# Attention scores on one core: TensorE's unrolled program becomes a loop over two tiles, with operands copied to fixed places by GpSimd

## The chip, the cores and the metric

The kernel runs on one core of a Trainium2 chip. A core has a matrix engine (TensorE, PE in the profile; PEld is its weight load), VectorE (DVE), ScalarE (ACT), GpSimd (POOL) and SyncE (SP), which here only issues transfers and passes counts on. Sixteen DMA engines move data between the chip's memory (HBM) and the core's on-chip memory SBUF. PE writes its results to a second on-chip memory, PSUM. The engines run programs of their own and wait for each other through semaphores, which are counters. The metric is the time of one execution in microseconds on the device, lower is better.

## The reference

```python
batch, heads, seq, dim = 8, 8, 512, 64
def reference(q, k):
    scale = 1.0 / np.sqrt(q.shape[-1])
    return (np.einsum('bhqd,bhkd->bhqk', q, k) * scale).astype(np.float32)
```

For each of 64 heads, the 512x64 queries are multiplied by the 512x64 keys, transposed, and scaled. The inputs are 16.8 MB in float32 and the output is 67.1 MB in float32, so the kernel reads little and writes much.

## The kernel before

**Units, chunks and tiles.** The eight batches are taken two at a time, in four *units* v. A unit's keys and queries are one load of 2 MB each (x = 0 for keys, x = 1 for queries). A unit has four *chunks* c: two of keys, two of queries, eight 128x128 blocks each, which PE transposes. A unit also gives four *tiles* g of output, 4 MB each: 16 tiles in all, and 16 chunks in all.

**The stages.** SP issues the loads into three large buffers, `bigs` (`load`, lines 81 and 82; the very first load is cut in two halves, one of them issued by ACT). POOL casts a loaded half-block from float32 to bfloat16 into `xb`, a ring of 12 chunk places (line 131; 16 casts of 128x2048). The bfloat16 pairs are then treated as float32 words, so that a transpose moves two values at once. PE transposes chunk c with an identity matrix as the moving operand into the PSUM tile `tp` (`turn`, line 139). ACT and DVE move the transposed chunk into `kT` (keys) and `qz` (queries, with zeros around them), each one half of the partitions in two copies (`move`, line 193). Both have places for two units.

**A tile.** `scores(g, p)` is one pair of matmuls (line 154): 128 query rows against 512 keys, bfloat16, into one of three PSUM buffers `pss`, taken in turn by the running number of the pair. A tile has eight pairs p. ACT takes the even pairs out of PSUM, DVE the odd ones, both multiplying by the scale, into the store buffer (lines 218 and 221, 128x1024 each). SP waits until both are through with the tile (line 101) and stores it (line 102). The store buffers are the same three `bigs` that the loads use.

**Order on PE.** The program is written out in full: four transposed chunks first, then 16 tiles. In tile g, after three pairs, PE transposes chunk g + 4 (there are 12 such chunks), then comes back to the other five pairs. Every matmul's addresses are written into its instruction: the place in `qz` and `kT` by g modulo 8, the PSUM buffer by the pair's number modulo 3. The second matmul of a tile's first pair waits for the store that last used the tile's output buffer, or, for the first three tiles, until POOL has cast what the buffer still holds:

```python
if g < 3:
    pe.wait_ge(sem["ready"], (2, 6, 8)[g])
else:
    pe.wait_ge(store_sems[g % 3], g // 3 * 16)
```

**What is counted.** `ready` counts pairs of casts, `turn` transposed chunks, `moved` the copies out of `tp`, `pe_act` and `pe_dve` pairs finished by PE, `act` and `dve` pairs taken out. A pair waits for the pair three before it to have left PSUM.

Of the kernel before, what the change touches and what calls it, by code (L numbers as in the profile page):

```python
# [5 lines left out]
def kernel(  # L6
# [5 lines left out]
    nc = tc.nc  # L12
    B, H, S, D = q.shape
    scale = 1.0 / (D ** 0.5)
    P = 128
    UNITS = B // 2
    N = H
    M = P // (2 * H)
    R = S // M
    J = R // 2  # L20
    RO = 8
    U = S // RO
    JP = J // 2
    JJ = J // RO // 2
    W = 8
    IW = W // JJ
    TILES = N // 2
    CHUNKS = 4
    SLOTS = 12
    PAIRS = RO  # L30

    f32 = mybir.dt.float32
    bf16 = mybir.dt.bfloat16
    mult = mybir.AluOpType.mult


    names = ["ready", "moved", "zeroed", "ident", "turn", "pe_act", "pe_dve", "act", "dve"]
    sem = {name: nc.alloc_semaphore(name) for name in names}
    load_sems = [nc.alloc_semaphore(f"load{n}") for n in range(2 * UNITS)]
    halves = [load_sems[0], nc.alloc_semaphore("load0b")]  # L40
    store_sems = [nc.alloc_semaphore(f"store{n}") for n in range(3)]
    ALL = CHUNKS * UNITS
# [2 lines left out]
    k_r = k.rearrange("(v b) g (m j) d -> v (b g m) (j d)", b=2, j=R)  # L45
    out_r = out.rearrange("(v b) (t x h) (u i) k -> (v b t) (h u) x (i k)", b=2, x=2, h=2, i=RO)

    bigs = [nc.alloc_sbuf_tensor(f"big{n}", [P, 2, RO, S], f32)[:] for n in range(3)]
    xb = nc.alloc_sbuf_tensor("xb", [P, SLOTS * W, 2, D, 2], bf16)[:]
    kT = nc.alloc_sbuf_tensor("kT", [P, 2 * N, M, 2, J], bf16)[:]  # L50
    qz = nc.alloc_sbuf_tensor("qz", [P, 2 * N, RO, P], bf16)[:]
    identity = nc.alloc_sbuf_tensor("identity", [P, P], f32)[:]
    tp = nc.alloc_psum_tensor("tp", [P, W, P], f32)[:]
    pss = [nc.alloc_psum_tensor(f"ps{n}", [P, 2, S], f32)[:] for n in range(3)]

    def words(ap):
        return ap.bitcast(f32)

    def half(h):
        return slice(h * D, (h + 1) * D)  # L60

    kw = words(kT)
    qw = words(qz)
    xw = words(xb.rearrange("p w s d e -> p w (s d e)"))
    keys = kT.rearrange("p n m s j -> p n (m s j)")

    pe = nc.tensor

    def xf(v):
        return bigs[(0, 1, 2, 1)[v]].rearrange("p x i k -> p (x i k)").rearrange(
            "p (x s c) -> p x s c", x=2, s=2)

    def store_buffer(g):
        return bigs[(0, 2, 1)[g % 3]]

    def rows(v, x):
        return (k_r, q_r)[x][v].rearrange("p (s c) -> p s c", s=2)

    def load(v, x):
        nc.sync.dma_start(out=xf(v)[:, x], in_=rows(v, x)).then_inc(load_sems[2 * v + x], 16)
# [8 lines left out]
    tc.compile()  # L91


    for n in range(1, 2 * (UNITS - 1)):
        load(n // 2, n % 2)
    for x in range(2):
        nc.sync.wait_ge(sem["ready"], 3 + x)
        load(UNITS - 1, x)
    for g in range(ALL):
        nc.sync.wait_ge(sem["act"], 4 * g + 4)  # L100
        nc.sync.wait_ge(sem["dve"], 4 * g + 4)  # L101
        nc.sync.dma_start(out=out_r[g], in_=store_buffer(g).rearrange("p x i k -> p x (i k)")
                          ).then_inc(store_sems[g % 3], 16)
    for n in range(3):
        nc.sync.wait_ge(store_sems[n], 16 * len(range(n, ALL, 3)))


    nc.gpsimd.memset(identity, 0.0).then_inc(sem["ident"], 1)  # L108
# [2 lines left out]
                            fill=1.0, base=0, pattern=[[-1, P]], channel_multiplier=1  # L111
                            ).then_inc(sem["ident"], 1)
    for v in range(UNITS):
        for x in range(2):
            w0 = (v * CHUNKS + 2 * x) % SLOTS * W
            if v or x:
                nc.gpsimd.wait_ge(load_sems[2 * v + x], 16)
            if v == UNITS - 1 and x == 0:
                nc.gpsimd.wait_ge(sem["turn"], CHUNKS)
            for s in range(2):  # L120
                if v == x == 0:
                    nc.gpsimd.wait_ge(halves[s], 16)
                src = xf(v)[:, x, s]
                dst = xb[:, w0:w0 + JP, s]
                if x == 0:
                    src = src.rearrange("p (j e d) -> p j e d", e=2, d=D)
                    dst = dst.rearrange("p j d e -> p j e d")
                else:
                    src = src.rearrange("p (j e i d) -> p j e i d", e=2, i=RO, d=D)
                    dst = dst.rearrange("p (i j) d e -> p j e i d", i=RO)  # L130
                cast = nc.gpsimd.tensor_copy(out=dst, in_=src)  # L131
            cast.then_inc(sem["ready"], 1)


    first = [tp] + [ps.rearrange("p w (c k) -> p (w c) k", k=P) for ps in pss]

    def turn(c, dst):
        for w in range(W):
            ins = pe.transpose(out=dst[:, w], identity=identity, in_=xw[:, c % SLOTS * W + w])  # L139
        ins.then_inc(sem["turn"], 1)  # L140

    def scores(g, p):
        x, i = p // 4, p % 4 * 2
        n = g % (2 * TILES) * 2 + x
        pair = PAIRS * g + p
        if pair >= 3:
            pe.wait_ge(sem["act" if p % 2 else "dve"], (pair - 3) // 2 + 1)
        for w in range(2):
            if p == 0 and w == 1:
                if g < 3:  # L150
                    pe.wait_ge(sem["ready"], (2, 6, 8)[g])
                else:
                    pe.wait_ge(store_sems[g % 3], g // 3 * 16)
            ins = pe.matmul(out=pss[pair % 3][:, w, :], lhsT=qz[:, n, i + w], rhs=keys[:, n],  # L154
                            start=True, stop=True)
        ins.then_inc(sem["pe_dve" if p % 2 else "pe_act"], 1)

    pe.wait_ge(sem["ident"], 2)
    for c in range(CHUNKS):
        if c % 2 == 0:  # L160
            pe.wait_ge(sem["ready"], c // 2 + 1)
        turn(c, first[c])
    pe.wait_ge(sem["moved"], 4 * CHUNKS)
    for g in range(ALL):
        c = g + CHUNKS
        for p in range(3):
            scores(g, p)
        if c < ALL:
            pe.wait_ge(sem["ready"], c // 2 + 1)
            turn(c, tp)  # L170
        for p in range(3, PAIRS):
            scores(g, p)
        if c < ALL:
            pe.wait_ge(sem["moved"], 4 * c + 4)

    def move(copy, c, s, tile_):
        v, t = divmod(c, CHUNKS)
        n0 = v % 2 * N  # L180
        h0 = t % 2 * W
        if t < 2:
            src = tile_[half(s)].rearrange("d j (n h m) -> d h n m j", n=N, h=2)
        else:
            src = tile_[half(s)].rearrange("d (i jj) (n h m) -> d h i n m jj", jj=JJ, n=N, h=2)
            h0 = t % 2 * IW
        for h in range(2):
            if t < 2:
                dst = kw[half(h), n0:n0 + N, :, s, h0:h0 + W]
            else:  # L190
                dst = qw[half(h), n0:n0 + N, h0:h0 + IW, h * U // 2:(h + 1) * U // 2].rearrange(
                    "d n i (m s jj) -> d s i n m jj", s=2, jj=JJ)[:, s]
            copy(out=dst, in_=src[:, h]).then_inc(sem["moved"], 1)  # L193

    def evacuator(engine, copy, scaled, parity, done, freed):
        if parity:
            for v in range(2):
                engine.memset(qz[:, v * N:(v + 1) * N], 0.0).then_inc(sem["zeroed"], 1)  # L198
        for c in range(CHUNKS):
            engine.wait_ge(sem["turn"], c + 1)  # L200
            if c == 2:
                engine.wait_ge(sem["zeroed"], 2)
            move(copy, c, parity, first[c])
        count = 0
        for g in range(ALL):
            o = store_buffer(g)
            for p in range(parity, PAIRS, 2):
                x, i = p // 4, p % 4 * 2
                count += 1
                engine.wait_ge(done, count)  # L210
                scaled(o[:, x, i:i + 2, :], pss[(PAIRS * g + p) % 3]).then_inc(freed, 1)
                c = g + CHUNKS
                if p in (1, 2) and c < ALL:
                    engine.wait_ge(sem["turn"], c + 1)
                    move(copy, c, parity, tp)

    evacuator(nc.scalar, nc.scalar.copy,
              lambda o, ps: nc.scalar.mul(out=o, in_=ps, mul=scale),  # L218
              0, sem["pe_act"], sem["act"])
    evacuator(nc.vector, nc.vector.tensor_copy,  # L220
              lambda o, ps: nc.vector.tensor_scalar(out=o, in0=ps, scalar1=scale, scalar2=None,  # L221
                                                    op0=mult),
              1, sem["pe_dve"], sem["dve"])


# [28 lines left out]
```

## Time and profile before

| | us |
|---|---|
| median of 5 runs | 201.21 (201.12 to 201.32) |
| the profiled execution's own time | 201.28 |
| its span, first to last instruction | 200.0 |
| PE busy in matmuls (384) | 101.2 |
| DVE busy (98 instructions) | 106.0 |
| ACT busy (97) | 84.8 |
| POOL busy (22) | 39.4 |
| DMA, mean over the span | 420 GB/s, 83.95 MB |

The profile's first part gives each engine's busy time, the second cuts the span into 40 slices of 5 us and gives busy tenths of each engine and of the 16 DMA engines together. The third lists the DMA queues: each line has a queue's packets, its megabytes and the time of its packets as a share of 16 engines' span. Queue q1 holds what SP issued, q10 what ACT issued, and the queues marked "instruction" fetch program code. The other parts list groups of instructions with their mean duration and what ended the idle time before them, waits, and DMA issues. The same questions can be put to any stretch of the span; "marks" below are the small completion packets that each transfer leaves, one for each DMA engine.

### The profile page before, as it was taken

What the parts mean: (1) busy time and instruction counts of PE and PEld (TensorE: products, weight loads), DVE (VectorE), ACT (ScalarE), POOL (GpSimd) and SP (SyncE); (2) the same over time, 40 slices, a digit from 0 to 9 for tenths busy, and PEclk for the clock granted to TensorE, in tenths of its full rate; (3) what the DMA queues carried; (4) which work ended last, traced back from release to release, by engine and by line L of the source; (5) the groups of instructions that cost most, each with busy time, mean ns of one, the idle gap of its engine ahead of it and who ended that gap; (6) DMA issues with size and microseconds to landing.
All of it is one profiled execution on the core that took longest, in us unless ns stands there. A gap on an engine that the chain in (4) does not pass through costs nothing.

```text
span 200.0 us, 1082 instructions
## 1 busy us (share of the span) xinstructions
PE 101.2 (51%) x384; PEld 47.3 (24%) x384; DVE 106.0 (53%) x98; ACT 84.8 (42%) x97; POOL 39.4 (20%) x22
## 2 busy tenths in 40 slices
PE   0027660476875767654764587365737373830000
PEld 0036430143331424312431333041202020200000
DVE  4815691176895847691769276829364544450000
ACT  2004670265693646562665366446444343430000
POOL 1299999996000000000000000000000000000000
PEclk9999997579797888995899579969696968585555
DMA  5999999999999999999999999999999999999995
GB/s 195 451 426 436 426 423 439 426 390 433 436 436 423 429 434 438 423 423 439 423 433 429 433 436 433 426 429 436 433 429 419 436 433 433 426 423 439 433 433 256
DMA packets 5653, 83.95 MB, mean 420 GB/s; under 512 B 400, under 2 KB 400, under 8 KB 400
## 3 DMA queue, kind: packets, MB, share of 16 engines
q1 hardware_dynamic: 5504, 82.84, 97.3%
q10 hardware_dynamic: 144, 1.05, 1.3%
q8 instruction: 3, 0.05, 0.1%
q14 instruction: 2, 0.02, 0.0%
HBM read 16.78 MB, written 67.11 MB: 419 GB/s over the span
## 4 chain that ended last, share of the span: by engine, by line
DMA 56%; DVE 12%; PE 10%; POOL 10%; issue 1%; SPq 0%
DMA out_dram<-big 42%; DMA big<-in_q_dram 13%; POOL xb L131 10%; DVE big L221 10%; PE ps L154 7%; PE tp L139 3%; DVE qz L193 2%; DVE kT L193 1%; SPq L101 0%
## 5 line engine op out<-in xcount | busy, mean ns | idle before, releaser
L154 PE MATMUL ps<-kT,qz 128*128 128x512 bf16 x256 | 81.0, 454 | 60.6 <-DMA out_dram<-big 30.7
L221 DVE TENSOR_SCALAR big<-ps 128x1024 f32<-128x1024 f32 x64 | 76.9, 1222 | 52.4 <-PE ps L154 51.9
L218 ACT ACTIVATE big<-ps 128x1024 f32<-128x1024 f32 x64 | 65.0, 1023 | 71.3 <-PE ps L154 70.9
L154 PEld LDWEIGHTS ps<-kT,qz 128*128 128x128 bf16 x256 | 25.1, 110 | 109.6 <-DMA out_dram<-big 34.4
L131 POOL CAST xb<-big 128x2048 bf16<-128x2048 f32 x16 | 38.7, 2464 | 6.6 <-DMA big<-in_k_dram 5.9
L139 PE MATMUL tp<-identity,xb 128*128 128x128 f32 x104 | 19.2, 347 | 13.5 <-POOL xb L131 13.5
L139 PEld LDWEIGHTS tp<-identity,xb 128*128 128x128 f32 x104 | 17.5, 187 | 17.5 <-issue 16.3
L193 DVE COPY kT<-tp 64x512 f32<-64x512 f32 x14 | 9.7, 694 | 9.8 <-PE tp L139 9.4
L193 ACT COPY kT<-tp 64x512 f32<-64x512 f32 x14 | 8.1, 577 | 14.4 <-PE tp L139 14.1
L193 DVE COPY qz<-tp 64x512 f32<-64x512 f32 x12 | 8.3, 695 | 3.8 <-PE tp L139 3.4
L198 DVE MEMSET qz<- 128x4096 uint32 x2 | 6.9, 3472 | 3.6 <-PEq L91 2.8
L193 ACT COPY qz<-tp 64x512 f32<-64x512 f32 x12 | 7.4, 618 | 1.7 <-PE tp L139 1.6
L139 PE MATMUL ps<-identity,xb 128*128 128x128 f32 x24 | 5.6, 423 | 1.2 <-POOL xb L131 1.2
L139 PEld LDWEIGHTS ps<-identity,xb 128*128 128x128 f32 x24 | 5.0, 229 | 1.6 <-POOL xb L131 1.6
L193 DVE COPY qz<-ps 64x512 f32<-64x512 f32 x4 | 2.8, 695 | 2.1 <-PE ps L139 2.0
L193 ACT COPY qz<-ps 64x512 f32<-64x512 f32 x4 | 2.5, 625 | 2.5 <-PE ps L139 2.4
L193 ACT ACT_TABLE_LOAD x1 | 1.3, 1283 | 1.9 <-PEq L91 1.9
L193 DVE COPY kT<-ps 64x512 f32<-64x512 f32 x2 | 1.4, 694 | 0.3 <-PE ps L139 0.3
L193 ACT COPY kT<-ps 64x512 f32<-64x512 f32 x2 | 1.2, 578 | 0.5 <-PE ps L139 0.5
L108 POOL MEMSET identity<- 128x128 f32 x1 | 0.2, 204 | 1.5 <-POOLq L91 1.5
L110 POOL TENSOR_SCALAR_AFFINE_SELECT identity<-identity 128x128 f32<-128x128 f32 x1 | 0.3, 292 | 0.2 <-POOL identity L108 0.2
L238 POOL MEMSET const-float32-0.0<- 128x1 f32 x1 | 0.1, 98 | 0.2 <-issue 0.2
(3 smaller groups left out, 0.3 us busy)
## 6 DMA issues: line engine op xcount, KB each, us to landing
out_dram<-big SPq DMA_DIRECT2D x16, 4096.0 KB, 21.3
big<-in_q_dram SPq DMA_DIRECT2D x4, 2048.0 KB, 17.6
big<-in_k_dram SPq DMA_DIRECT2D x3, 2048.0 KB, 16.0
big<-in_k_dram ACTq DMA_DIRECT2D x1, 1024.0 KB, 7.9
big<-in_k_dram SPq DMA_DIRECT2D x1, 1024.0 KB, 7.8
```

Source lines behind the costliest of these rows:

```text
L108: nc.gpsimd.memset(identity, 0.0).then_inc(sem["ident"], 1)
L110: nc.gpsimd.affine_select(out=identity, in_=identity, compare_op=mybir.AluOpType.not_equal, fill=1.0, base=0, pattern=[[-1, P]], channel_m ...
L131: cast = nc.gpsimd.tensor_copy(out=dst, in_=src)
L139: ins = pe.transpose(out=dst[:, w], identity=identity, in_=xw[:, c % SLOTS * W + w])
L154: ins = pe.matmul(out=pss[pair % 3][:, w, :], lhsT=qz[:, n, i + w], rhs=keys[:, n], start=True, stop=True)
L193: copy(out=dst, in_=src[:, h]).then_inc(sem["moved"], 1)
L198: engine.memset(qz[:, v * N:(v + 1) * N], 0.0).then_inc(sem["zeroed"], 1)
L218: lambda o, ps: nc.scalar.mul(out=o, in_=ps, mul=scale),
L221: lambda o, ps: nc.vector.tensor_scalar(out=o, in0=ps, scalar1=scale, scalar2=None, op0=mult),
L238: nc = _bacc.Bacc("TRN2", target_bir_lowering=False, num_devices=1)
```

## The change

PE's 16 tiles become a loop of 8 rounds over two tiles (`pe.Fori`). The instructions in the loop have fixed addresses, so what they read must lie where they look:

- `kT` and `qz` become one tensor `kq` with 20 places; each holds a tile half's keys and queries together (512 + 1024 bfloat16 in each partition). The first four are the fixed places, two for each of the two tiles in the loop. Units 0 and 2 are moved to the places from 0 on, units 1 and 3 to those from 12 on. So the first two tiles are already in place; every later tile's two places are copied into the fixed ones (`fix`, 128x3072 bfloat16): tile 2's by ACT, tiles 3 to 15 by POOL. A fix waits until PE has finished the tile two before, and, for a unit's first tile, until that unit is moved.
- Chunks to transpose in the loop are read from `xs`, two chunk places. Chunks 4 and 5 are cast straight into `xs`; chunks 6 to 15 are cast into `xb` (10 places now) and copied by POOL (`fill`, 128x2048 bfloat16) once the chunk two before has been transposed. An `If` in the loop leaves the transposes out in the last four tiles.
- A pair's PSUM buffer is now its number within the tile modulo 3, so a tile's first pairs wait for the last ones of the tile before, by way of SP.
- PE's waits use counts that it takes down again itself. The start of each tile is one count, `next`, which SP gives: after issuing store g it waits for the casts (tiles 1 and 2) or for the store that last used the next buffer, and for the fix, and then lets PE begin tile g + 1. Store g itself now waits for `out`, which ACT and DVE raise with their last pair of a tile.
- Unit 3's first load waits for one cast more than before (the first half of unit 1's queries).
- `moved` is raised once by each engine for each unit, and PE no longer waits for it within the tiles; the fix does.

```diff
-            ins = pe.transpose(out=dst[:, w], identity=identity, in_=xw[:, c % SLOTS * W + w])
+            if take and w == 0:
+                pe.wait_ge(sem["ready"], 1)
+            ins = pe.transpose(out=dst[:, w], identity=identity, in_=src[:, w])
+            if take and w == 1:
+                ins.then_inc(sem["ready"], -1)
...
-    for g in range(ALL):
-        c = g + CHUNKS
-        for p in range(3):
-            scores(g, p)
-        if c < ALL:
-            pe.wait_ge(sem["ready"], c // 2 + 1)
-            turn(c, tp)
-        for p in range(3, PAIRS):
-            scores(g, p)
-        if c < ALL:
-            pe.wait_ge(sem["moved"], 4 * c + 4)
+    with pe.Fori(0, ALL // 2) as two:
+        for t in range(2):
+            for p in range(3):
+                scores(t, p)
+            with pe.If(two < (ALL - CHUNKS) // 2):
+                turn(xsw[:, t * W:(t + 1) * W], tp, True)
+            for p in range(3, PAIRS):
+                scores(t, p)
...
+    def fill(c):
+        nc.gpsimd.wait_ge(sem["turn"], c - 1)
+        nc.gpsimd.tensor_copy(
+            out=xs[:, c % 2 * W:(c % 2 + 1) * W].rearrange("p w s d e -> p (w s d e)"),
+            in_=xb[:, slot(c) * W:(slot(c) + 1) * W].rearrange("p w s d e -> p (w s d e)")
+        ).then_inc(sem["ready"], 1)
+
+    def fix(copy, g):
+        v, t = divmod(g, TILES)
+        n = place(v) + 2 * t
+        return copy(out=kq[:, g % 2 * 2:g % 2 * 2 + 2].rearrange("p n c -> p (n c)"),
+                    in_=kq[:, n:n + 2].rearrange("p n c -> p (n c)"))
+
+    fill(CHUNKS + 2)
+    for g in range(3, ALL):
+        if g + CHUNKS < ALL:
+            fill(g + CHUNKS)
+        if g % TILES == 0:
+            nc.gpsimd.wait_ge(sem["moved"], 2 * (g // TILES + 1))
+        nc.gpsimd.wait_ge(sem["pe_dve"], PAIRS // 2 * (g - 1))
+        fix(nc.gpsimd.tensor_copy, g).then_inc(sem["fixed"], 1)
...
     for x in range(2):
-        nc.sync.wait_ge(sem["ready"], 3 + x)
+        nc.sync.wait_ge(sem["cast"], 1 + x)
         load(UNITS - 1, x)
     for g in range(ALL):
-        nc.sync.wait_ge(sem["act"], 4 * g + 4)
-        nc.sync.wait_ge(sem["dve"], 4 * g + 4)
+        nc.sync.wait_ge(sem["out"], 2 * g + 2)
         nc.sync.dma_start(out=out_r[g], in_=store_buffer(g).rearrange("p x i k -> p x (i k)")
                           ).then_inc(store_sems[g % 3], 16)
+        if g < ALL - 1:
+            if g < 2:
+                nc.sync.wait_ge(sem["cast"], 3 + g)
+            else:
+                nc.sync.wait_ge(store_sems[(g + 1) % 3], 16 * ((g + 1) // 3))
+            if g == 1:
+                nc.sync.wait_ge(sem["second"], 1)
+            elif g > 1:
+                nc.sync.wait_ge(sem["fixed"], g - 1)
+            nc.sync.sem_inc(sem["next"], 1)
```

## The prediction

> **What bounds the kernel now.** I read the page's DMA rows first, then the waits, then the last microseconds by stretches. The slices and the queue table (queue, packets, MB, share of the 16 engines' time):
>
> ```profile
> DMA  5999999999999999999999999999999999999995
> ...
> q1 hardware_dynamic: 5504, 82.84, 97.3%
> q10 hardware_dynamic: 144, 1.05, 1.3%
> q8 instruction: 3, 0.05, 0.1%
> q14 instruction: 2, 0.02, 0.0%
> ```
>
> The 16 DMA engines are full from the second slice to the last but one; the busiest compute engine, DVE, has 53%. 83.9 MB in 200.0 us is the bound, and no compute edit matters unless it starves the stores. But the kernel ends when its *last* DMA engine ends, and here they part (columns: stretch, length, PE, PEld, DVE, ACT, POOL, clock, DMA share, GB/s):
>
> ```profile
> 197.00:197.50 0.50, 0.00 (x0) 0.00 (x0) 0.00 (x0) 0.00 (x0) 0.00 (x0) 0.50 1.15 492
> 197.50:198.00 0.50, 0.00 (x0) 0.00 (x0) 0.00 (x0) 0.00 (x0) 0.00 (x0) 0.50 0.54 229
> 198.00:198.50 0.50, 0.00 (x0) 0.00 (x0) 0.00 (x0) 0.00 (x0) 0.00 (x0) 0.50 0.23 98
> 198.50:199.00 0.50, 0.00 (x0) 0.00 (x0) 0.00 (x0) 0.00 (x0) 0.00 (x0) 0.50 0.23 98
> ```
>
> A share of 0.23 is about 4 engines of 16. Every DMA leaves one small packet under 512 B on each of its 16 engines when it is through (400 in all, 25 DMAs), so counting these in a stretch says how many engines have finished. For the last store, 197.7 to 198.3, then 198.3 to 198.9 us, then 199.4 to 199.55:
>
> ```profile
> DMA packets 16, 0.07 MB, mean 109 GB/s; under 512 B 12, under 2 KB 12, under 8 KB 12
> ...
> DMA packets 4, 0.07 MB, mean 109 GB/s; under 512 B 0, under 2 KB 0, under 8 KB 0
> ...
> DMA packets 2, 0.00 MB, mean 0 GB/s; under 512 B 2, under 2 KB 2, under 8 KB 2
> ```
>
> Twelve are through by 198.3 (the last mark at 198.28), the others at 199.00, 199.13, 199.46 and 199.50. The tail is 1.2 us, with bandwidth idle. Its cause shows where the first of the three 16 KB packets of the instruction queue q8 falls: 51.7 to 52.5 us, where store 0 lands, then 52.5 to 53:
>
> ```profile
> DMA packets 38, 0.38 MB, mean 471 GB/s; under 512 B 15, under 2 KB 15, under 8 KB 15
> ...
> q8 instruction: 1, 0.02, 7.5%
> ...
> DMA packets 12, 0.18 MB, mean 360 GB/s; under 512 B 1, under 2 KB 1, under 8 KB 1
> ```
>
> Stores land every 9.72 us on each engine. The mark due at 51.90 came at 52.85, and in the next store at 62.94 where 61.62 was due: the fetch put its engine back 1.32 us, for good (16 marks between 41.9 and 42.8, before any fetch, lie within 0.72). The other two are at 97.0 and 150.8 us; after the third, 4 marks of store 11 come later than 159.5. PE had run 97, 217 and 337 matmuls by 52.0, 97.1 and 150.9: 120 apart, so q8 follows PE's program. The two 8 KB packets of q14 (74.4 and 75.5 us, ACT and DVE then at equal counts) moved marks by only 0.3 to 0.5 us.
>
> What can starve the stores is read from the waits:
>
> ```profile
> SPq L101 <- DVE big L221: 143.0, 16, 15.6
> ...
> PE ps L154 <- DMA out_dram<-big: 30.7, 12, 4.0
> ```
>
> SP issues the stores at 31.05, 47.0, 56.1, 62.7 us and so on, well before the queue needs them, and PE itself idles 1.3 to 4.0 us ahead of each of the last 12 tiles until a buffer has landed.
>
> **The change part by part.** *PE's program.* Before: 384 matmuls written out. After: 32 transposes and one loop body of 2 x 24, so 80, fewer than the 97 at which the first fetch came. If fetches follow the place in the program, all three go and the last mark falls from 199.50 to the 198.28 of the engines without one: -1.22 us. From below: one fetch kept (at the loop's end, or behind it) ends at 197.5 to 198.2 (the marks due without fetches, from 42.01 to 42.73 plus 16 x 9.72) plus 1.32, so 198.8 to 199.6: -0.7 to +0.1.
>
> [...]
>
> *Loop and branch stalls on PE* have no row. From below 0; from above 10 us: tile g starts when store g-3 lands, lasts 7.2 to 9.1 us (82.79 to 89.99; 92.49 to 101.58), and is needed 19.4 us after its start. All of that lies beside the stores. I take 0.
>
> *Order of starts.* PE's own wait for a store becomes SP's, then a count to PE. After the issue of store g, SP stands waiting for store g-2; behind it is only store g+1, whose tile cannot be ready before. A hop costs 0.02 to 0.05 us in the chain; hidden. Unit 3's first load waits a cast longer (issue 25.7 instead of 23.2); the queue needs it at about 31, when its predecessor lands. Hidden.
>
> *POOL's copies:* 10 fills of 128x2048 and 13 fixes of 128x3072, bf16 to bf16. Nearest row:
>
> ```profile
> L131 POOL CAST xb<-big 128x2048 bf16<-128x2048 f32 x16 | 38.7, 2464 | 6.6 <-DMA big<-in_k_dram 5.9
> ```
>
> 1.20 ns an element: 2.46 and 3.70 us, 6.2 per tile against 9.72 per store. Bounds: half for half the input bytes (0.6), and 2.3 (the 128x128 affine select, 292 ns with its fixed part). I take 1.2, the same engine and size. On the path at the start: casts end at 48.0, fill 6 at 50.5, so tile 2's transposes start 1.6 us later than at 48.92 and store 2 issues at 57.7 (needed by about 60.4, 1 us ahead of store 1's first mark). Fill 7 to 53.0, fix 3 to 56.7, tile 3 from 57.9 to 67.0 at most (needed by 70.2). Fill 8 to 59.2, unit 1's last move at 62.9, fix 4 to 66.6, tile 4 done 76.2 (79.9). Later tiles gain about 0.6 us each. Margins of 2.7 us and more: cost 0. With fixes in the way of nothing else, POOL's bound is crossed at 1.9 ns (5120 elements in 9.72 us), and tile 3's at 1.8.
>
> *ACT's one fix* (3.1 us by 1.02 per 1024, 3.6 by the 64x512 copies) lies in ACT's idle 8.2 us before 38.5. *DVE's memsets* cover 10 places instead of 8 each: 3.47 to 4.3 us, done by 13 where DVE's next work is at 15.5; even at twice that, store 0 has 10 us to spare.
>
> *POOL's and SP's longer programs* may each fetch one more small block: ACT and DVE did near their 48th record; POOL had 36 in all and gets over 23 more. 0 to 0.5 us each, only where it hits one of the last engines; I take +0.15 together.
>
> Sum, against the profiled run's 201.28 (span 200.0, the rest around it): -1.22 + 0.15 = -1.07. The five runs' median is 201.21, 0.07 lower, so 200.15.
>
> [...]
>
> **Rivals.** *One fetch stays* (for: PE's program with what surrounds it could just reach the next block; against: 80 against 97 matmuls): 198.8 to 199.6 as last mark, 200.5 to 201.3, middle 200.8. *Nothing moves* (fetches counted by instructions run, or the late engines late for other reasons; for: the engine with the mark at 199.00 also drifted by 0.15 us a store from 100 to 140 us): 201.2. [...] *POOL the bound:* at 2.3 ns, 11.8 us a tile, 2.1 us lost for each of nine tiles and 1 to 3 at the start, 220; it needs 1.8 ns, and the cast has 1.2.
>
> **How the numbers follow.** All fetches gone, nothing starved: 0.55, 199.7 to 200.7. One stays: 0.16, mostly faster. Nothing moves: 0.07. Refetching: 0.15, 201.2 to 203. POOL or an unforeseen stall at the start: 0.07, above 203. The runs lie within 0.2 us, so 0.2% (0.4 us) is about what can be told from no change. Faster: 0.55 + 0.13 = 0.68; same 0.03 + 0.07 + 0.02 = 0.12; slower 0.20. The range leaves out the upper half of refetching, POOL, and little below: 199.6 to 202.2; the likeliest case alone 199.7 to 200.7.
>
> **What would show it.** Right: no q8 packets behind the start, 16 marks of the last store within 0.9 us, DMA share 9 throughout, POOL busy about 112 us, stores 2 and 3 issued near 57.7 and 67. Wrong: q8 packets at each return (refetching), a DMA slice under 9 after 45 us (starved), or a tail of several engines with no fetch before it.

## The result, and the profile after

The changed kernel takes 201.44 us (median of 30 runs, 201.30 to 202.13), the kernel before 201.22 us (median of 51). The ratio is 1.0011, with a 95% interval of 1.0006 to 1.0016. It is slower by 0.11% (0.22 us, by the interval 0.12 to 0.32), and I had forecast 200.15 us, faster by 0.5%. The profiled run took 201.60 us, with a span of 200.3.

The page of the changed kernel, its slices of DMA and its queues (queue, packets, MB, share of 16 engines' time):

```profile
span 200.3 us, 1154 instructions
...
DMA  5999999999999999999999999999999999999995
...
q1 hardware_dynamic: 5504, 82.84, 97.2%
q10 hardware_dynamic: 144, 1.05, 1.3%
q14 instruction: 2, 0.02, 0.0%
```

The line of q8 is gone: TensorE's loop fetches no program code during the run, as forecast (the two 8 KB packets of q14 are there as before). The DMA engines are full from the second slice to the last but one, so nothing starved either. The end, by stretches (stretch, length, five engines' busy time, clock, DMA share, GB/s):

```profile
197.00:197.50 0.50, 0.00 (x0) 0.00 (x0) 0.00 (x0) 0.00 (x0) 0.00 (x0) 0.50 1.07 459
197.50:198.00 0.50, 0.00 (x0) 0.00 (x0) 0.00 (x0) 0.00 (x0) 0.00 (x0) 0.50 0.39 164
198.00:198.50 0.50, 0.00 (x0) 0.00 (x0) 0.00 (x0) 0.00 (x0) 0.00 (x0) 0.50 0.01 0
198.50:199.00 0.50, 0.00 (x0) 0.00 (x0) 0.00 (x0) 0.00 (x0) 0.00 (x0) 0.50 0.08 33
199.00:199.50 0.50, 0.00 (x0) 0.00 (x0) 0.00 (x0) 0.00 (x0) 0.00 (x0) 0.50 0.08 33
```

Where the kernel before had about four DMA engines at work behind 198.0, a share of 0.08 is about one of sixteen, and it works alone for 1.5 us. The marks of the last store, 197.8 to 198.4, 198.4 to 199.7, and 199.7 to 199.9:

```profile
DMA packets 16, 0.02 MB, mean 27 GB/s; under 512 B 15, under 2 KB 15, under 8 KB 15
...
DMA packets 2, 0.03 MB, mean 25 GB/s; under 512 B 0, under 2 KB 0, under 8 KB 0
...
DMA packets 1, 0.00 MB, mean 0 GB/s; under 512 B 1, under 2 KB 1, under 8 KB 1
```

Fifteen engines are through by 198.34, close to the 198.28 where I had put the last one. The sixteenth ends at 199.80, later than the last of before (199.50). It falls behind slowly. At store 2 (71.1 to 71.8 us) all marks lie together; at store 7 (119.7 to 120.7, then 120.7 to 121.3) one is apart:

```profile
DMA packets 38, 0.36 MB, mean 515 GB/s; under 512 B 16, under 2 KB 16, under 8 KB 16
...
DMA packets 44, 0.48 MB, mean 475 GB/s; under 512 B 15, under 2 KB 15, under 8 KB 15
...
DMA packets 17, 0.26 MB, mean 437 GB/s; under 512 B 1, under 2 KB 1, under 8 KB 1
```

I followed the latest mark from store to store in the trace's DMA records. A step of an undisturbed engine is 9.72 us in both traces. In the trace of before, a slow engine's marks can be followed once one knows to look for it; there they are not the latest of every store, since the engines with a fetch lie beside it:

| store | after: mark, step (us) | before: mark, step (us) |
|---|---|---|
| 6 | 111.35, 9.89 | 111.14, 9.87 |
| 7 | 121.23, 9.88 | 121.01, 9.86 |
| 8 | 131.10, 9.87 | 130.89, 9.88 |
| 9 | 141.00, 9.90 | 140.76, 9.87 |
| 10 | 150.84, 9.84 | 150.58, 9.82 |
| 11 | 160.67, 9.83 | 160.40, 9.82 |
| 12 | 170.50, 9.83 | 170.21, 9.81 |
| 13 | 180.36, 9.86 | 180.06, 9.85 |
| 14 | 190.08, 9.72 | 189.78, 9.72 |
| 15 | 199.80, 9.72 | 199.50, 9.72 |

Both kernels have one slow engine. It loses 0.09 to 0.18 us a store while the compute engines run, and nothing once they are done (PE's last tile is at 171 to 177 us). In the kernel before, its slow engine set the end, at 199.50, only just ahead of the engines that the code fetches had put back (199.46, 199.13, 199.00). Taking those away bared it.

GpSimd's copies were cheaper than I had taken them. The groups of the two copies (busy, mean ns of one, then idle time before them):

```profile
L177 POOL COPY kq<-kq 128x3072 bf16<-128x3072 bf16 x13 | 35.7, 2751 | 49.5 <-DVE kq L250 31.1
...
L169 POOL COPY xs<-xb 128x2048 bf16<-128x2048 bf16 x10 | 18.9, 1902 | 9.1 <-PE tp L199 9.1
```

### The profile page after: what moved, and what is told of

It reads as the page before. It is cut to its first block, busy times and chain, and to the rows that moved or that the text cites. A ratio compares the mean times of both kernels' runs of the same rounds, so it can differ in the third digit from the quotient of the medians.

```text
span 200.3 us, 1154 instructions
## 1 busy us (share of the span) xinstructions
PE 100.7 (50%) x384; PEld 47.7 (24%) x384; DVE 107.9 (54%) x98; ACT 87.7 (44%) x98; POOL 93.5 (47%) x45
## 4 chain that ended last, share of the span: by engine, by line
DMA 45%; DVE 17%; PE 14%; POOL 11%; issue 1%; SPq 1%
DMA out_dram<-big 32%; DVE big L291 13%; DMA big<-in_q_dram 13%; PE ps L211 10%; POOL xb L157 7%; DVE kq L250 4%; PE tp L199 3%; POOL xs L157 2%; POOL xs L169 1%; SPq L116 1%; SPq L127 0%
## 5 line engine op out<-in xcount | busy, mean ns | idle before, releaser
L211 PE MATMUL ps<-kq 128*128 128x512 bf16 x256 | 80.8, 464 | 61.8 <-SPq L127 43.6
L288 ACT ACTIVATE big<-ps 128x1024 f32<-128x1024 f32 x64 | 65.0, 1024 | 69.9 <-PE ps L211 69.4
L177 POOL COPY kq<-kq 128x3072 bf16<-128x3072 bf16 x13 | 35.7, 2751 | 49.5 <-DVE kq L250 31.1
L211 PEld LDWEIGHTS ps<-kq 128*128 128x128 bf16 x256 | 25.9, 111 | 109.4 <-issue 67.0
L250 DVE COPY kq<-tp 64x512 f32<-64x512 f32 x26 | 18.0, 694 | 11.2 <-PE tp L199 10.7
L169 POOL COPY xs<-xb 128x2048 bf16<-128x2048 bf16 x10 | 18.9, 1902 | 9.1 <-PE tp L199 9.1
L250 ACT COPY kq<-tp 64x512 f32<-64x512 f32 x26 | 15.6, 599 | 15.5 <-PE tp L199 15.2
L199 PE MATMUL tp<-identity,xs 128*128 128x128 f32 x96 | 16.7, 332 | 0.1
L199 PEld LDWEIGHTS tp<-identity,xs 128*128 128x128 f32 x96 | 15.5, 180 | 4.7 <-issue 3.3
L199 PE MATMUL tp<-identity,xb 128*128 128x128 f32 x8 | 1.9, 424 | 13.5 <-POOL xb L157 13.5
L199 PEld LDWEIGHTS tp<-identity,xb 128*128 128x128 f32 x8 | 1.6, 224 | 13.5 <-issue 13.5
```

The lines of the kernel that those rows point to most:

```text
L169: nc.gpsimd.tensor_copy(out=xs[:, c % 2 * W:(c % 2 + 1) * W].rearrange("p w s d e -> p (w s d e)"), in_=xb[:, slot(c) * W:(slot(c) + 1) * ...
L177: return copy(out=kq[:, g % 2 * 2:g % 2 * 2 + 2].rearrange("p n c -> p (n c)"), in_=kq[:, n:n + 2].rearrange("p n c -> p (n c)"))
L199: ins = pe.transpose(out=dst[:, w], identity=identity, in_=src[:, w])
L211: ins = pe.matmul(out=pss[p % 3][:, w, :], lhsT=qz[:, n, i + w], rhs=keys[:, n], start=True, stop=True)
L250: last = copy(out=dst, in_=src[:, h])
```

## The experiments

Theory D, formed on these two traces: one DMA engine loses time with the compute engines' instructions and alone sets the end; the fetches delay other engines, which have time to spare. Theory F, that of the prediction: the fetches set the end, and the loop has a new cost of the same size somewhere.

**The loop written out again.** The copies, the waits and the fixed places stay.

```diff
-    with pe.Fori(0, ALL // 2) as two:
+    for two in range(ALL // 2):
...
-            with pe.If(two < (ALL - CHUNKS) // 2):
+            if two < (ALL - CHUNKS) // 2:
```

> The changed kernel with TensorE's loop written out again, all copies and waits kept. Theory D (one DMA engine loses about 0.15 us a store while the compute engines run, and it alone sets the end; fetches of program code delay other engines that had 1.2 us to spare): the three 16 KB code packets come back, four marks of the last store again lie later than 198.4 us, but the last mark stays near 199.5 to 199.9, so the time is 201.3 to 201.6, the same as with the loop (201.44) within 0.15. Theory F (as I predicted: the code fetches set the end, and the loop took something of the same size elsewhere): 1.2 us more than with the loop, 202.6.

It took 201.32 us, 1.0003 times the kernel before (0.9993 to 1.0012). Its queue of code, and the marks of its last store at 197.7 to 198.3 and at 198.3 to 199.6:

```profile
q8 instruction: 3, 0.05, 0.1%
...
DMA packets 16, 0.07 MB, mean 109 GB/s; under 512 B 12, under 2 KB 12, under 8 KB 12
...
DMA packets 7, 0.05 MB, mean 38 GB/s; under 512 B 4, under 2 KB 4, under 8 KB 4
```

The three fetches and the four late engines are back, the last at 199.49, and the time is not above that of the loop. Here the last two end together: by their marks the slow engine is through at 199.47 and one with a fetch at 199.49. So the fetches are worth nothing to this time; theory F, which expected 202.6, falls.

**More instructions on GpSimd**, each of one element, behind each copy.

```diff
         fix(nc.gpsimd.tensor_copy, g).then_inc(sem["fixed"], 1)
+        for n in range(16 * g, 16 * g + 16):
+            nc.gpsimd.memset(scratch[:, n:n + 1], 0.0)
```

> The changed kernel with 16 more GpSimd instructions (one-element memsets of unused memory) behind each of the 13 copies, 208 in all, no DMA changed. Theory D with the loss going by the number of instructions: at 5 to 10 ns each 1 to 2 us more, 202.4 to 203.5, all of it in the last mark of one DMA engine, the other fifteen within 198.4. If the loss goes by another thing (time, TensorE's work, bytes copied): 201.4.

It took 201.98 us (1.0034, 1.0023 to 1.0045): 0.54 more than the changed kernel, 2.6 ns for each of the 208. The direction is that of theory D, the size is about half of the least that I expected (1 to 2 us). The group, and the marks of the last store at 197.8 to 198.6 and at 200.3 to 200.5:

```profile
L190 POOL MEMSET scratch<- 128x1 f32 x208 | 7.8, 99 | 0.0
...
DMA packets 17, 0.03 MB, mean 41 GB/s; under 512 B 15, under 2 KB 15, under 8 KB 15
...
DMA packets 1, 0.00 MB, mean 0 GB/s; under 512 B 1, under 2 KB 1, under 8 KB 1
```

208 instructions that occupy GpSimd for 7.8 us, move no data by DMA and make nobody wait lengthen the kernel, and all of it lies on one DMA engine (200.44), the other fifteen at 198.51 or before. Busy time is not what counts: the change keeps GpSimd busy 54 us longer than before for 0.22 us, these memsets 7 us longer for 0.54.

**Four tiles instead of sixteen.** TensorE, VectorE, ScalarE and GpSimd stop after tile 3; the other stores still send 4 MB each.

```diff
+    LIVE = 4
...
-    with pe.Fori(0, ALL // 2) as two:
+    with pe.Fori(0, LIVE // 2) as two:
...
-        for g in range(ALL):
+        for g in range(LIVE):
             o = store_buffer(g)
```

> The changed kernel with the work of tiles 4 to 15 left out (TensorE, VectorE, ScalarE and GpSimd do tiles 0 to 3 only; the other twelve stores send what lies in the buffers, each after the store three before it). Theory D: the one engine loses nothing after about 70 us, the sixteen last marks lie within 1 us, the last near 198.4, time 200.0 to 200.3. If the slow engine is slow whatever the compute engines do: 201.4.

It took 199.97 us (0.9933, 0.9916 to 0.9950). A stretch behind the last tile, and the marks of the last store at 197.7 to 198.3:

```profile
75.00:100.00 25.00, 0.00 (x0) 0.00 (x0) 0.00 (x0) 0.00 (x0) 0.00 (x0) 0.50 1.00 431
...
DMA packets 16, 0.00 MB, mean 0 GB/s; under 512 B 16, under 2 KB 16, under 8 KB 16
```

With idle compute engines the sixteen DMA engines end together, the last at 198.25. The same bytes at the same rate are through 1.5 us earlier. Theory D holds: the slow engine is slow because of what the compute engines do.

**More instructions on TensorE**, a short matmul ahead of every full one.

```diff
+            pe.matmul(out=pss[p % 3][:, w, :32], lhsT=qz[:, n, i + w], rhs=keys[:, n, :32],
+                      start=True, stop=True)
             ins = pe.matmul(out=pss[p % 3][:, w, :], lhsT=qz[:, n, i + w], rhs=keys[:, n],
```

> The changed kernel with one more short matmul (32 columns, overwritten by the full one) ahead of every full matmul, 256 weight loads and 256 matmuls more, no DMA changed. Theory D with the loss going by every instruction, TensorE's too: at 2 to 3 ns each 1 to 1.5 us more, 202.4 to 203. If TensorE's instructions don't count: 201.4, unless the tiles at the start come too late, which would show as DMA slices under 9.

It took 202.55 us (1.0064, 1.0047 to 1.0081), 1.11 more than the changed kernel for 512 instructions more, 2.2 ns each. TensorE's instructions count like GpSimd's. The last mark, at 200.6 to 200.7, and the DMA queues from 42.5 to 43.5 us, which show something else:

```profile
DMA packets 1, 0.00 MB, mean 0 GB/s; under 512 B 1, under 2 KB 1, under 8 KB 1
...
DMA packets 29, 0.44 MB, mean 442 GB/s; under 512 B 2, under 2 KB 2, under 8 KB 2
...
q8 instruction: 1, 0.02, 5.8%
```

One engine is last again, at 200.63; the engine of the one code fetch is through at 199.66, the other fourteen at 198.81 or before. This loop's body is longer by 64 instructions a round, and code is fetched once in the whole run, in the first round (tile 1 runs then); not once a round.

Set side by side, the instructions that the page counts and the time over the kernel before of the same call, the five runs lie near one line:

| kernel | instructions, against 1082 | time against before (us) | ns each |
|---|---|---|---|
| four tiles | 429, -653 | -1.29 | 2.0 |
| loop written out | 1106, +24 | +0.06 | 2.5 |
| the change | 1154, +72 | +0.22 | 3.1 |
| more on GpSimd | 1354, +272 | +0.72 | 2.6 |
| more on TensorE | 1634, +552 | +1.29 | 2.3 |

The page lacks 2, 7, 8 and 16 matmul records in the first, second, fourth and fifth row; with them the last column reads 2.0, 1.9, 3.1, 2.6 and 2.3. In the first row the other engines set the end, so it is a lower bound. The two small rows are near the noise: the interval of the second holds 0, that of the third goes from 1.7 to 4.5 ns. The change's 72 are 41 of TensorE's branches, moves and additions for the loop, 4 more of its waits, 26 on GpSimd (23 copies, 3 waits) and 1 on ScalarE.

**Relieving the slow engine.** If it could send less, both kernels should gain. I cut the last stores so that some rows go as transfers of their own, over fewer DMA engines. First, the last two stores, in both kernels:

```diff
+            nc.sync.dma_start(out=out_r[g][:, 0], in_=src[:, 0]).then_inc(store_sems[g % 3], 16)
+            nc.sync.dma_start(out=out_r[g][:112, 1], in_=src[:112, 1]).then_inc(parts[3 * (g % 2)], 16)
+            nc.sync.dma_start(out=out_r[g][112:127, 1], in_=src[112:127, 1]).then_inc(parts[3 * (g % 2) + 1], 16)
+            nc.sync.dma_start(out=out_r[g][127:, 1].rearrange("p (a b) -> p a b", a=16),
...
```

> The changed kernel, with the last two stores each cut in four: the first halves of all 128 rows, the second halves of rows 0 to 111, of rows 112 to 126 (15 rows), and of row 127 in 16 pieces. If a transfer of 15 rows uses 15 of the 16 DMA engines and the slow engine is the one left out, it sends 2 packets of 0.61 us less, its last mark falls from 199.8 to 198.6, and the time from 201.44 to 200.2 to 200.4. If the slow engine is another one: 201.4 to 201.5, and one engine's last mark near 197 instead.

> The kernel before, with the same cut of its last two stores. If the slow engine is relieved, the engines that the three code fetches put back (last marks 199.0 to 199.46) are what is left, so the gain is 0 to 0.3 us: 200.9 to 201.25. Together with the changed kernel cut likewise this shows what the loop is worth once the slow engine no longer sets the end: theory D says 0.6 to 1.0 us. If code fetches cost nothing at all, both cut kernels take the same time.

They took 207.57 us (1.0306, 1.0273 to 1.0339) and 206.86 us (1.0295, 1.0272 to 1.0317), so neither theory's number came. Row 127 did not go in 16 pieces: the trace has no packet of 1 KB, and its 464 marks instead of 400 are 16, 15 and 1 more for each of the two stores, so this row went through one engine. Stretches of the first run:

```profile
188.00:190.00 2.00, 0.00 (x0) 0.00 (x0) 0.00 (x0) 0.00 (x0) 0.00 (x0) 0.50 1.25 279
190.00:196.00 6.00, 0.00 (x0) 0.00 (x0) 0.00 (x0) 0.00 (x0) 0.00 (x0) 0.50 0.90 341
...
203.00:206.00 3.00, 0.00 (x0) 0.00 (x0) 0.00 (x0) 0.00 (x0) 0.00 (x0) 0.50 0.12 49
```

From where the cut stores begin, the DMA engines are as busy as before but move 279 to 341 GB/s instead of 430, and they end up to 6 us apart (all sixteen work until 200.0, the last until 206.1). Here a transfer of 112 rows did not go like seven eighths of one of 128. That the rows then meet other engines on the way is my guess; no run separates it. The two runs say nothing on the slow engine.

Then only the last store, with far less data in the pieces, and one run with even pieces beside it to price the cut itself:

```diff
+            nc.sync.dma_start(out=out_r[g][:, 0], in_=src[:, 0]).then_inc(store_sems[g % 3], 16)
+            for n, (rows_, cols) in enumerate(((slice(0, P), slice(0, 3072)),
+                                               (slice(0, 120), slice(3072, 4096)),
+                                               (slice(120, P), slice(3072, 4096)))):
...
```

> The changed kernel; only the last store is cut: first halves of all rows, 12 KB of the second halves of all rows, then the last 4 KB of rows 0 to 119 and, by itself, of rows 120 to 127. Far less data (0.5 MB) than before changes its DMA engine. If 120 rows use 15 engines and the slow engine is the sixteenth, it sends 32 KB less, 1.2 us, and the time is 200.2 to 200.5. If the slow engine is another one: 201.4 to 201.7, and one engine is through near 197.

> The kernel before with the same cut. If the slow engine is relieved, the engines put back by code fetches remain (last marks 199.0 to 199.5): 200.9 to 201.3, so the loop is worth 0.6 to 1.0 us here. If the slow engine is another one: 201.2 to 201.5.

> The changed kernel with the last store cut in three pieces of all 128 rows (16, 12 and 4 KB a row), so every DMA engine sends as much as uncut. It shows what the cutting alone costs: 201.4 to 201.6 by every theory; above 201.8 the cutting itself costs, and the run with uneven pieces has to be read against this one.

They took 201.85 us (1.0032, 1.0021 to 1.0044), 202.04 us (1.0037, 1.0023 to 1.0051) and 201.55 us (1.0017, 1.0008 to 1.0026). Cutting alone costs 0.1 us, and the uneven pieces bring a loss, not a gain: the first two runs lie above both of their expected ranges, so they don't show what the loop would be worth with the slow engine relieved. In the records of the first, the slow engine finishes its 12 KB pieces at 198.48, and from there a row of 4 KB packets runs without a gap to 199.89: nine of them at 0.156 us, eight of the 120 rows and one of the eight. It was not left out.

Last, the ends of the rows as 119, 7 and 2 rows:

```diff
+            for n, (rows_, cols) in enumerate(((slice(0, P), slice(0, 3584)),
+                                               (slice(0, 119), slice(3584, 4096)),
+                                               (slice(119, 126), slice(3584, 4096)),
+                                               (slice(126, P), slice(3584, 4096)))):
...
```

> The changed kernel; the last store's last 2 KB of every row are sent by themselves, as 119, 7 and 2 rows, the earlier part by all 128 rows. [...] If 119 and 7 rows use only the first seven DMA engines and the slow one is the eighth, the slow one sends 16 KB less (0.6 us), the first seven 20 KB more (0.8 us on top of 198.3): last mark 199.0 to 199.2, time 200.8 to 201.1, which would beat both kernels. If the slow engine is one of the first seven, it ends 0.8 us later: 202.1 to 202.4.

It took 202.57 us (1.0062, 1.0049 to 1.0076), the second of the two expected outcomes, somewhat above it. The slow engine's last 14 KB packet ends at 199.23, and eighteen 2 KB packets of 0.08 us follow to 200.69. So in both cuts the transfers of few rows loaded the slow engine rather than sparing it, and I found no complete version that beats the kernel before.

## Why the prediction was wrong

**The fetches: the mechanism was right, the sum was not.** The step that failed is "all three go and the last mark falls from 199.50 to the 198.28 of the engines without one: -1.22 us". All three went, and the engines that they had put back came in by 198.34. But I had put all four late engines of the old tail down to fetches, of which there were three. The fourth was the slow engine, and it was the last. The true term is 0, as the run with the loop written out shows: it has all three fetches and takes no more than the loop. I had seen its drift "from 100 to 140 us", tied it to the mark at 199.00, and gave the rival "Nothing moves" 0.07. That rival was right in its second form, late for other reasons. The time lies within my wide range, 199.6 to 202.2, but that reached up for a fetch that stays and for refetching, neither of which came; it says nothing for the mechanism.

**The term that I didn't have** is +0.22 us, for 72 more instructions at about 3 ns on the slow engine. By the 2.2 and 2.6 ns of the runs with more instructions they make 0.16 to 0.19 us, within the interval of 0.12 to 0.32. The prediction priced added instructions by engine time, waits and code blocks, all of which were hidden or absent; a price for each instruction on a DMA engine has no row in the page. The trace of before shows the engine that pays it once its marks are followed; what it pays for, only the experiments show.

**Small code blocks of GpSimd and SP:** taken as +0.15; none came (q14 has 2 packets, as before). With 208 more on GpSimd there were 4.

**POOL's copies:** taken as 2.46 and 3.70 us, measured 1.90 and 2.75, 0.9 ns an element instead of 1.2, between the bounds of 0.6 and 2.3. The cast row that I let decide lay too high. A copy differs from the cast in its two-byte input and in its plain order of elements; no run separates the two. It did no harm, since POOL was never the bound; busy 93.5 us against the forecast 112.

**The starts:** store 2 was issued at 55.87 (forecast 57.7), store 3 at 65.53 (at most 67.0), unit 3's first load at 25.77 (25.7), always before the queue needed them. SP's hop to TensorE takes 0.17 us in the chain (0.03 on SP, 0.14 before the first matmul), more than the 0.02 to 0.05 that I took, and hidden. ScalarE's fix took 2.74 us (taken as 3.1 to 3.6), DVE's memsets 4.33 each, as taken. Unit 2, by the way, is moved to the places from 4 on, not from 0: places 0 to 3 are the fixed ones.

**The loop and refetching:** the returns to the loop's head take 0.21 to 0.22 us on TensorE's sequencer, the `If` 0.07 to 0.08 where the transposes run and 0.20 to 0.21 where it jumps over them, all beside the stores; TensorE fetched no code (no packet on q8). Refetching, to which the forecast gives 0.15 and 201.2 to 203, was my supposition that each return to the loop's head fetches code again; no run shows such a fetch. In its place, the changed kernel made its seven returns without one, and the longer body, in the run with more matmuls, brought one fetch of 16 KB in eight rounds, at 42.5 to 43.5 us.

## What to carry to other kernels

This kernel, its DMA engines full from the second slice to the last but one, ended with its last DMA engine, and several delays of one size ended there together (before, the slow engine's at 199.50 and those of the fetches at 199.46, 199.13 and 199.00). In another such kernel, count the causes against the late engines, and follow the last mark back store by store before crediting it to a cause: here, removing the second-latest thing gained nothing (201.32 us with the three fetches, 201.44 without). Instructions were not free even on engines that were not the bound: as these runs were measured, each cost 2 to 3 ns at the end of the kernel, so the extra copies, branches and waits, which saved nothing else, were a loss of 0.22 us. The transfers of 112 rows did not go like those of 128 (279 to 341 GB/s instead of 430), and cutting the last one unevenly to remove its tail of 1.5 us made the kernel 0.4 and 1.1 us longer instead.

## What the runs showed of the hardware that I had not expected

- One DMA engine of the sixteen lost time for instructions executed on the compute engines, 2.2 ns for each of 512 of TensorE's and 2.6 for each of 208 of GpSimd's, and no engine fell behind when they stood still (sixteen last marks within 0.5 us, 199.97 us with four tiles against 201.44). In the traces before and after, 9 to 16 of its sixteen 16 KB packets a store took 612 to 644 ns instead of 611 while the compute engines ran, in the stores where they can be followed one by one. What goes through that engine is open. The timed runs list a span and a clock as the profiled one does, so no run tells whether the loss is there when nothing is recorded.
- Which engine it is, is open too; no run here shows how the engines are numbered. The marks show only how many engines a transfer of few rows used: the run with 119, 7 and 2 rows has 432 marks instead of 400, 16 more for the piece of all rows and 7, 7 and 2 for the others, and the slow engine took part in it with eighteen packets of 2 KB.
- Each of the three 16 KB code fetches of the kernel before put its DMA engine back by about two data packets of 0.61 us, for the rest of the run: marks due at 61.62, 100.62 and 159.21 us came at 62.94, 101.95 and 160.59 (1.32, 1.33 and 1.37 later). Each fell on another engine, by the last marks at 199.00, 199.13 and 199.46.
